# Two halves of the tokens in turn: the order of matmuls in the split products of a decoder trunk

## The chip, the cores and the metric

The kernel runs on one core of one Trainium2 chip. The metric is the device time of one execution in microseconds (us), lower is better; the median of several runs is given. The profile is one execution taken by the hardware profiler. TensorE (PE in the rows, PEld for its weight loads) multiplies, VectorE (DVE), ScalarE (ACT) and GpSimd (POOL) do the rest, SyncE (SP) issues most transfers.

## What is computed

Two residual layers over 256 tokens of 2048 features, all in float32. Cut to the parts that matter here:

```
for l in range(2):
    shift1, scale1, gate1, shift2, scale2, gate2 = split(silu(c) @ ada_w[l] + ada_b[l], 6)
    h = rms(x, norm1_g[l]) * (1 + scale1) + shift1
    mix = even_mixer(h) if l == 0 else mla_mixer(h)     # each with an input and an output projection
    x = x + gate1 * mix
    h = rms(x, norm2_g[l]) * (1 + scale2) + shift2
    x = x + gate2 * (square(relu(h @ mlp_w1[l])) @ mlp_w2[l])    # 2048 -> 8192 -> 2048
```

## The kernel before

Tokens are taken as two halves (`NH = 2`) of 128, the partitions of a PSUM tile; a product gives `[256, 512]` as two PSUM tiles of 128 x 512, one bank for each half. The features that are summed over come in blocks of 128.

**Split products.** From the even layer's output projection on, every product of activations and weights is made of three matmuls per block, half and chunk: both operands are split into a high and a low part (`split`, L93), and high x high, high x low and low x high are added in the same bank. A weight tile of four blocks x 512 columns (1 MiB) is fetched by SyncE (`wraw`, L112), copied to its high part by ScalarE (L94) and subtracted to its low part by VectorE (L95), or by GpSimd for a few tiles at the start of a stage (`self.first`). Three buffers hold high parts, two hold low parts. The even layer's input projection uses whole float32 passes instead (`gemm32`, L148).

**Order of the matmuls.** `gemm_part` (L172) takes one weight tile (or two). Its outer loop is over the halves of the tokens; inside, the four blocks, and for each block the three products at L183 (high x high), L184 (the same block of x with the low part of the weights) and L185 (low part of x, high part of the weights). So twelve matmuls add to the first half's bank and then twelve to the second's. `gemm` (L162) runs it for a whole sum. With `skew` the last two tiles go together, 24 matmuls for the first half and then 24 for the second; that is used at the last chunk of the two MLPs and of the odd layer's output projection (`at_end`, L319). With `between` (the query product, L847) other work stands between the two halves. At the start of an MLP, `gemm_quarter` (L190) and `unit_halves` (L201, products at L210 to L212) add a quarter of the features to three chunks as soon as the modulation has made that quarter; for the first quarter two chunks go together, first half first.

**Around it.** After a unit of 512 hidden channels the MLP takes relu (L452, ScalarE), a product (L454, VectorE), four transposes on TensorE (L107) and a split, for each half. After an output projection comes the residual (L411, L412), the sum of squares (L340), the norm (L345 to L354), transposes and the modulation (L380 to L383), which gives the next product's x. In the odd layer the query input's rows are squared (L656), normalized (L672) and modulated into `cT` (L678). Beside all this the conditioning is worked off step by step on VectorE (L237, L269, L297), as `side_work` (L136) doles it out per weight tile. PSUM has four banks for running sums (two units), two for transposes and two for other uses; at the start of an MLP these last two hold the third chunk.

The framework puts the instructions of each engine into a queue when the kernel is built, by the order in which they are written and by when it expects their inputs; the engine then takes its queue as it is.

Of the kernel before, what the change touches and what calls it, by code (L numbers as in the profile page):

```python
# [16 lines left out]
P = 128  # L17
# [25 lines left out]
class Trunk:  # L43
    def __init__(self, ctx, tc, t):
# [17 lines left out]
        self.first = 0  # tiles still to be split by GpSimd  # L62
# [5 lines left out]
    def rsqrt(self, out, v):  # L68
        """out = v ** -0.5 for v > 0: a first guess from the bits, a third-order step, a Newton step."""
# [14 lines left out]
        # out <- 8/3 of its third-order step, then Newton with the 8/3 taken out again  # L84
# [7 lines left out]
    def split(self, src, hi, lo, engine=None):  # L92
        """src = hi + lo, both with the 12 significant bits that one pass of the array takes."""  # L93
        self.nc.scalar.copy(hi, src)  # L94
        (engine or self.nc.vector).tensor_tensor(lo, src, hi.bitcast(F32), op=ALU.subtract)  # L95
# [6 lines left out]
    def transpose4(self, srcs):  # L102
        """Up to four [128, n] blocks -> one PSUM bank, transposed side by side."""
# [20 lines left out]
    def wtile(self, w, k0, nk, n0, nw):  # L124
# [3 lines left out]
        # VectorE is busy with the norm when a phase's first tiles come: GpSimd splits those  # L128
# [6 lines left out]
    def side_work(self, size=1.0):  # L135
        """Work that is spread beside the weight tiles: conditioning and the convolution."""  # L136
# [10 lines left out]
    def gemm32(self, ps, x, w, g, n0):  # L147
        """ps += x[:, 512 features of group g] @ w[those, n0:n0+512], whole float32 passes."""  # L148
# [12 lines left out]
    def gemm(self, x, xk0, w, k0, nkb, n0, nw, skew=False):  # L161
        """[256, nw] = x[:, K] @ w[K, n0:n0+nw], as two PSUM tiles of 128 tokens; with skew the  # L162
        first half of the tokens is complete well before the second."""
# [7 lines left out]
    def gemm_part(self, ps, x, xk0, w, k0, g, nkb, n0, nw, tiles=1, between=None):  # L171
        nc = self.nc  # L172
        xh, xl = x
        ws = [self.wtile(w, k0 + g + 4 * i, min(4, nkb - g - 4 * i), n0, nw) for i in range(tiles)]
        for h in range(NH):
            o = ps[h][:, :nw]
            for k in range(g, min(g + 4 * tiles, nkb)):
                first, last = k == 0, k == nkb - 1
                hi, lo = ws[(k - g) // 4]
                i = (k - g) % 4  # L180
                a = xh[:, xk0 + k, h * P : (h + 1) * P]
                b = xl[:, xk0 + k, h * P : (h + 1) * P]
                nc.tensor.matmul(o, a, hi[:, i, :nw], start=first, stop=False)  # L183
                nc.tensor.matmul(o, a, lo[:, i, :nw], start=False, stop=False)  # L184
                nc.tensor.matmul(o, b, hi[:, i, :nw], start=False, stop=last)  # L185
            if between and h == 0:
                between()

    def gemm_quarter(self, units, x, q, paired):
        """512 features of x into each of units = (psum, w, n0, nw); with paired, the first half of  # L190
        the tokens of two units goes before their second half."""
# [8 lines left out]
    def unit_halves(self, units, ws, x, q):  # L200
        nc = self.nc  # L201
        xh, xl = x
        for h in range(NH):
            for (ps, _, _, nw), (hi, lo) in zip(units, ws):
                o = ps[h][:, :nw]
                for i in range(4):
                    k = 4 * q + i
                    a = xh[:, k, h * P : (h + 1) * P]
                    b = xl[:, k, h * P : (h + 1) * P]
                    nc.tensor.matmul(o, a, hi[:, i, :nw], start=k == 0, stop=False)  # L210
                    nc.tensor.matmul(o, a, lo[:, i, :nw], start=False, stop=False)  # L211
                    nc.tensor.matmul(o, b, hi[:, i, :nw], start=False, stop=k == KB - 1)  # L212

# [1 line left out]
    # mod = silu(c) @ ada_w + ada_b, one 1 MiB piece of ada_w to a step  # L215
    def ada_finish_col(self, out, layer, j, q, acc):
        """Feature-major column sums of acc [128, 512], plus the bias."""
# [7 lines left out]
    def ada_col(self, layer, j):  # L225
        """self.mod[layer, j] = [128, 16], feature-major."""
# [19 lines left out]
    def ada_quarters(self, layer, j0, side=None, aided=0):  # L246
        """Columns j0 and j0 + 1 side by side, complete for 512 features after every eight steps.
        The first aided quarters go by ScalarE and GpSimd, with room for products in side."""
# [29 lines left out]
    def ada_row(self, layer, j, side=None):  # L278
        """self.mod[layer, j] = [128, 2048], the same in every partition. With side = [128, 4096],
        the products go to ScalarE and the sums to GpSimd."""  # L280
# [37 lines left out]
    def at_end(self, last):  # L318
        """Before the last product of a stage: no more work beside it."""  # L319
# [3 lines left out]
    def ada_more(self, rate, *lists):  # L323
        """Steps to be worked off beside the coming weight tiles, rate steps to a tile."""
# [26 lines left out]
    def norm_t(self, h, q, r):  # L351
        """Four blocks of (x * r).T in PSUM."""
# [4 lines left out]
    def norm_start(self, layer, which):  # L357
        """A function that gives 512 features' (shift, gain) columns: modulate(rms(x) * g) = x * rstd * gain + shift."""
# [14 lines left out]
    def norm_quarter(self, quarter, q, pair):  # L373
        """512 features of h.T, as (hi, lo)."""
# [649 lines left out]
```

## Time and profile before

| | |
|---|---|
| median of 3 runs | 2189.13 us (2187.72 to 2189.61) |
| span of the profiled execution, first to last instruction | 2185.9 us |
| what the median has beyond that span | 3.2 us |
| instructions in the span | 23655 |
| mean granted TensorE clock | 0.987 of 2.4 GHz |
| TensorE busy | 96% of the span |
| VectorE busy | 72% |
| ScalarE busy | 43% |
| read from HBM | 564.06 MB, 259 GB/s |

The profile gives the span of the profiled execution and no separate time for it, so the runs' median stands beside it. The stages in the span: conditioning and the even layer's input up to about 310 us, its output projection to 411, the first MLP to 1153, the odd layer to 1450, the second MLP to the end. TensorE's rows are matmuls with their start; they overlap, so a row's duration (0.39 us) is longer than the distance to the next start. A row of the timeline gives the start, the duration, the engine, the line, the operation and its tiles, and in brackets the idle time before it on its engine with what ended that.

### The profile page before, as it was taken

What the parts mean: (1) busy time and instruction counts of PE and PEld (TensorE: products, weight loads), DVE (VectorE), ACT (ScalarE), POOL (GpSimd) and SP (SyncE); (2) the same over time, 40 slices, a digit from 0 to 9 for tenths busy, and PEclk for the clock granted to TensorE, in tenths of its full rate; (3) what the DMA queues carried; (4) which work ended last, traced back from release to release, by engine and by line L of the source; (5) the groups of instructions that cost most, each with busy time, mean ns of one, the idle gap of its engine ahead of it and who ended that gap; (6) DMA issues with size and microseconds to landing.
All of it is one profiled execution on the core that took longest, in us unless ns stands there. A gap on an engine that the chain in (4) does not pass through costs nothing.

```text
span 2185.9 us, 23655 instructions
## 1 busy us (share of the span) xinstructions
PE 2090.9 (96%) x9138; PEld 1635.7 (75%) x9138; DVE 1564.9 (72%) x1763; ACT 932.3 (43%) x1184; POOL 146.7 (7%) x95
## 2 busy tenths in 40 slices
PE   2889999899999999999998999989999999999999
PEld 1444458678888888888888787868888888888887
DVE  6849999888777878787767878766656545554555
ACT  2135435444444334333436776444434433433432
POOL 0038710000000000000001000010000000000000
PEclk9999999899999999999999999989999999999999
DMA  9999968899898899989755646647778556556653
GB/s 350 384 346 330 332 242 295 275 317 339 315 337 315 329 326 319 339 304 334 270 174 174 211 158 214 229 154 250 256 271 264 178 192 189 189 192 192 189 191 122
DMA packets 238620, 567.70 MB, mean 260 GB/s; under 512 B 9150, under 2 KB 17784, under 8 KB 221864
## 3 DMA queue, kind: packets, MB, share of 16 engines
q1 hardware_dynamic: 236288, 562.60, 74.3%
q10 hardware_dynamic: 1564, 2.28, 0.3%
q8 instruction: 72, 1.18, 0.2%
q0 software_dynamic: 656, 1.31, 0.2%
q14 instruction: 40, 0.33, 0.0%
HBM read 564.06 MB, written 2.10 MB: 259 GB/s over the span
## 4 chain that ended last, share of the span: by engine, by line
PE 85%; DVE 9%; DMA 5%; ACT 1%; issue 1%; SPq 0%; ACTq 0%; DVEq 0%
PE mm L183 23%; PE mm L184 23%; PE mm L185 23%; PE mm L153 4%; DMA raw<-in_ada_w 4%; PE trp L107 3%; DVE accq L269 2%; DVE cvsq L542 1%; DVE wl L95 1%; PE mm L210 1%; PE mm L211 1%; PE mm L212 1%; PE sc L797 1%; PE sc L796 1%; DMA raw<-in_mlp_w 1%
## 5 line engine op out<-in xcount | busy, mean ns | idle before, releaser
L95 DVE TENSOR_TENSOR wl<-raw,wh 128x2048 fp32r<-128x2048 f32 (+2 forms) x312 | 704.7, 2259 | 424.0 <-PE mm L184 317.9
L94 ACT CAST wh<-raw 128x2048 fp32r<-128x2048 f32 (+3 forms) x316 | 596.6, 1888 | 774.1 <-PE mm L185 515.2
L183 PE MATMUL mm<-wh,f_h 128*128 128x512 f32 x1024 | 399.6, 390 | 0.0
L185 PE MATMUL mm<-wh,f_l 128*128 128x512 f32 x1024 | 399.3, 390 | 0.0
L184 PE MATMUL mm<-wl,f_h 128*128 128x512 f32 x1024 | 398.7, 389 | 0.0
L185 PE MATMUL mm<-wh,h_l 128*128 128x512 f32 (+2 forms) x928 | 358.2, 386 | 0.0
L183 PE MATMUL mm<-wh,h_h 128*128 128x512 f32 (+2 forms) x928 | 358.2, 386 | 0.0
L184 PE MATMUL mm<-wl,h_h 128*128 128x512 f32 (+2 forms) x928 | 357.0, 385 | 0.6 <-DVE wl L95 0.6
L185 PEld LDWEIGHTS mm<-wh,f_l 128*128 128x128 f32 x1024 | 192.2, 188 | 39.8
L184 PEld LDWEIGHTS mm<-wl,f_h 128*128 128x128 f32 x1024 | 192.3, 188 | 39.6
L183 PEld LDWEIGHTS mm<-wh,f_h 128*128 128x128 f32 x1024 | 192.3, 188 | 39.2
L184 PEld LDWEIGHTS mm<-wl,h_h 128*128 128x128 f32 x928 | 175.0, 189 | 34.0 <-DVE wl L95 1.1
L185 PEld LDWEIGHTS mm<-wh,h_l 128*128 128x128 f32 x928 | 174.9, 188 | 33.4
L183 PEld LDWEIGHTS mm<-wh,h_h 128*128 128x128 f32 x928 | 175.0, 189 | 32.7
L153 PE MATMUL mm<-raw,x 128*128 128x512 f32 x448 | 195.7, 596 | 1.0 <-ACT x L500 0.6
L269 DVE SCALAR_TENSOR_TENSOR accq<-raw,cT,accq 128x512 f32<-128x512 f32 x210 | 153.7, 749 | 16.6 <-DMA raw<-in_ada_w 13.3
L153 PEld LDWEIGHTS mm<-raw,x 128*128 128x128 f32 x448 | 84.6, 191 | 104.6 <-issue 98.5
L237 DVE SCALAR_TENSOR_TENSOR acc<-raw,cT,acc 128x2048 f32<-128x2048 f32 x60 | 140.8, 2346 | 9.7 <-DMA raw<-in_ada_w 9.7
L297 DVE SCALAR_TENSOR_TENSOR acc<-raw,cT,acc 128x2048 f32<-128x2048 f32 x48 | 112.7, 2347 | 4.4 <-DMA raw<-in_ada_w 4.4
L542 DVE SCALAR_TENSOR_TENSOR cvsq<-yp,convw,cvsq 128x256 f32<-128x256 f32 x240 | 96.0, 476 | 0.0
L303 POOL TENSOR_TENSOR side<-side 128x1024 f32<-128x1024 f32 x32 | 74.8, 2361 | 19.3 <-ACT side L302 19.3
L452 ACT ACTIVATE relu<-mm 128x512 f32<-128x512 f32 x60 | 35.8, 599 | 87.7 <-PE mm L185 81.5
(270 smaller groups left out, 2246.9 us busy)
## 6 DMA issues: line engine op xcount, KB each, us to landing
raw<-in_mlp_w SPq DMA_DIRECT2D x256, 1024.0 KB, 5.6
raw<-in_ada_w SPq DMA_DIRECT2D x192, 1024.0 KB, 5.4
raw<-in_ab_w_in SPq DMA_DIRECT2D x32, 1024.0 KB, 9.7
raw<-in_ab_w_out SPq DMA_DIRECT2D x16, 1024.0 KB, 8.3
raw<-in_mla_w_out SPq DMA_DIRECT2D x16, 1024.0 KB, 4.9
raw<-in_mla_w_ukv SPq DMA_DIRECT2D x8, 1024.0 KB
raw<-in_mla_w_uq SPq DMA_DIRECT2D x8, 768.0 KB, 4.8
raw<-in_mla_w_in SPq DMA_DIRECT2D x4, 1024.0 KB, 7.2
```

The costliest lines, as they stand in the source:

```text
L94: self.nc.scalar.copy(hi, src)
L95: (engine or self.nc.vector).tensor_tensor(lo, src, hi.bitcast(F32), op=ALU.subtract)
L107: self.nc.tensor.transpose(ps[:w, i * P : i * P + s.shape[0]], s, self.ident[: s.shape[0], : s.shape[0]])
L153: self.nc.tensor.matmul(ps[h], x[:, 4 * g + k, h * P : (h + 1) * P], raw[:, k, :], start=g + k == 0, stop=4 * g + k == KB - 1,)
L183: nc.tensor.matmul(o, a, hi[:, i, :nw], start=first, stop=False)
L184: nc.tensor.matmul(o, a, lo[:, i, :nw], start=False, stop=False)
L185: nc.tensor.matmul(o, b, hi[:, i, :nw], start=False, stop=last)
L237: nc.vector.scalar_tensor_tensor(acc, raw, self.cT[:, kb : kb + 1], acc, op0=ALU.mult, op1=ALU.add)
L269: self.last = nc.vector.scalar_tensor_tensor(acc, raw[:, k, :], c, acc, op0=ALU.mult, op1=ALU.add).ins
L297: nc.vector.scalar_tensor_tensor(acc, raw, c, acc, op0=ALU.mult, op1=ALU.add)
L303: nc.gpsimd.tensor_tensor(acc[:, sl], acc[:, sl], prod, op=ALU.add)
L542: nc.vector.scalar_tensor_tensor(o, y, wk, o, op0=ALU.mult, op1=ALU.add)
```

## The change

In `gemm_part` the loop over the halves moves inside the loop over blocks: for each block the three products are issued for both halves in turn. Where two tiles go together or something stands between the halves, the halves stay apart as before. `unit_halves` loops over the four blocks, then over the chunks, then over the products and halves, so the halves are in turn there too, also for the first quarter. A new function `products` holds the three products. Comments and docstrings are dropped in the changed file as well.

```diff
     def gemm_part(self, ps, x, xk0, w, k0, g, nkb, n0, nw, tiles=1, between=None):
-        nc = self.nc
-        xh, xl = x
         ws = [self.wtile(w, k0 + g + 4 * i, min(4, nkb - g - 4 * i), n0, nw) for i in range(tiles)]
-        for h in range(NH):
-            o = ps[h][:, :nw]
-            for k in range(g, min(g + 4 * tiles, nkb)):
-                first, last = k == 0, k == nkb - 1
-                hi, lo = ws[(k - g) // 4]
-                i = (k - g) % 4
-                a = xh[:, xk0 + k, h * P : (h + 1) * P]
-                b = xl[:, xk0 + k, h * P : (h + 1) * P]
-                nc.tensor.matmul(o, a, hi[:, i, :nw], start=first, stop=False)
-                nc.tensor.matmul(o, a, lo[:, i, :nw], start=False, stop=False)
-                nc.tensor.matmul(o, b, hi[:, i, :nw], start=False, stop=last)
-            if between and h == 0:
+        ks = range(g, min(g + 4 * tiles, nkb))
+        for halves in ([0], [1]) if between or tiles > 1 else ([0, 1],):
+            for k in ks:
+                hi, lo = (w[:, (k - g) % 4, :nw] for w in ws[(k - g) // 4])
+                self.products([ps[h][:, :nw] for h in halves], x, xk0 + k, hi, lo, halves, k == 0, k == nkb - 1)
+            if between and halves == [0]:
                 between()
 
+    def products(self, outs, x, k, hi, lo, halves, first, last):
+        for i, (a, w) in enumerate(((0, hi), (0, lo), (1, hi))):
+            for o, h in zip(outs, halves):
+                self.nc.tensor.matmul(
+                    o, x[a][:, k, h * P : (h + 1) * P], w, start=first and i == 0, stop=last and i == 2
+                )
+
...
     def unit_halves(self, units, ws, x, q):
-        nc = self.nc
-        xh, xl = x
-        for h in range(NH):
+        for i in range(4):
             for (ps, _, _, nw), (hi, lo) in zip(units, ws):
-                o = ps[h][:, :nw]
-                for i in range(4):
-                    k = 4 * q + i
-                    a = xh[:, k, h * P : (h + 1) * P]
-                    b = xl[:, k, h * P : (h + 1) * P]
-                    nc.tensor.matmul(o, a, hi[:, i, :nw], start=k == 0, stop=False)
-                    nc.tensor.matmul(o, a, lo[:, i, :nw], start=False, stop=False)
-                    nc.tensor.matmul(o, b, hi[:, i, :nw], start=False, stop=k == KB - 1)
+                k = 4 * q + i
+                outs = [ps[h][:, :nw] for h in range(NH)]
+                self.products(outs, x, k, hi[:, i, :nw], lo[:, i, :nw], range(NH), k == 0, k == KB - 1)
```

## Rows read from the trace of the kernel before

**Rows 1.** The page, part 1: busy us, share of the span and instructions of each engine

```profile
PE 2090.9 (96%) x9138; PEld 1635.7 (75%) x9138; DVE 1564.9 (72%) x1763; ACT 932.3 (43%) x1184; POOL 146.7 (7%) x95
```

**Rows 2.** Windows: stretch, its us, busy PE PEld DVE ACT POOL, clock, DMA, GB/s

```profile
411.00:422.50 11.50, 1.29 (x6) 0.74 (x5) 11.00 (x32) 5.11 (x10) 0.00 (x0) 0.67 0.97 330
414.95:428.60 13.65, 7.21 (x22) 5.68 (x23) 11.23 (x35) 7.04 (x15) 0.00 (x0) 0.50 0.78 247
508.00:1153.00 645.00, 645.00 (x2917) 533.10 (x2916) 499.46 (x326) 259.79 (x198) 6.96 (x7) 1.00 0.86 306
1532.00:2181.00 649.00, 649.00 (x2924) 536.24 (x2922) 355.87 (x231) 258.98 (x189) 0.00 (x0) 1.00 0.62 204
```

**Rows 3.** Groups of instructions: count, busy us, mean ns, idle before; two weight loads of the MLPs

```profile
L183 PEld LDWEIGHTS mm<-wh,f_h 128*128 128x128 f32 x1024 | 192.3, 188 | 39.2
L184 PEld LDWEIGHTS mm<-wl,f_h 128*128 128x128 f32 x1024 | 192.3, 188 | 39.6
```

**Rows 4.** Timeline of TensorE in the first MLP (start us, us, engine, line, operation)

```profile
797.64 0.39 PE L184 MATMUL mm<-wl,h_h 128*128 128x512 f32 x1
...
812.15 0.39 PE L185 MATMUL mm<-wh,h_l 128*128 128x512 f32 x1
812.37 0.39 PE L183 MATMUL mm<-wh,h_h 128*128 128x512 f32 x1
...
813.96 0.39 PE L184 MATMUL mm<-wl,h_h 128*128 128x512 f32 x1
```

**Rows 5.** Timeline of all engines there: relu of the first half, transposes of both

```profile
812.57 0.60 ACT L452 ACTIVATE relu<-mm 128x512 f32<-128x512 f32 x1 [4.61 <-PE mm L185]
...
815.33 0.60 PE L107 MATMUL trp<-ident,sq 128*128 128x128 f32 x4
...
820.12 0.60 PE L107 MATMUL trp<-ident,sq 128*128 128x128 f32 x4
```

**Rows 6.** Timeline, end of the even output projection and start of the first MLP

```profile
408.77 0.68 DVE L411 TENSOR_TENSOR rt<-mm,gate 128x512 f32<-128x512 f32 x1
...
410.79 0.39 PE L185 MATMUL mm<-wh,cat_l 128*128 128x512 f32 x1
...
419.13 1.08 PE L107 MATMUL trp<-ident,xn 128*128 128x128 f32 x4 [7.95 <-DVE nr L87]
...
422.48 0.80 PE L210 MATMUL mm<-wh,h_h 128*128 128x512 f32 x1 [2.26 <-DVE h_h L382]
...
426.19 0.43 DVE L382 CAST h_h<-full 128x512 fp32r<-128x512 f32 x1 [1.71 <-ACT full L380]
```

**Rows 7.** Groups of instructions on VectorE from 411 to 422.5 us

```profile
L269 DVE SCALAR_TENSOR_TENSOR accq<-raw,cT,accq 128x512 f32<-128x512 f32 x7 | 5.2, 747 | 0.0
```

**Rows 8.** Timeline, odd layer: square of the query input's first half, first query product

```profile
1215.60 0.60 ACT L656 ACTIVATE rj<-mm 128x512 f32<-128x512 f32 x1 [1.23 <-PE mm L185]
...
1228.19 0.44 PE L183 MATMUL mm<-wh,cT 128*128 128x384 f32 x1 [0.69 <-DVE cT L678]
```

**Rows 9.** Timeline, first MLP: the two waits for the low part of the weights

```profile
481.88 0.51 PE L211 MATMUL mm<-wl,h_h 128*128 128x512 f32 x1 [1.59 <-DVE wl L95]
...
507.35 0.50 PE L184 MATMUL mm<-wl,h_h 128*128 128x512 f32 x1 [0.64 <-DVE wl L95]
```

**Rows 10.** Timeline, start of the second MLP: first matmuls, cast of the second half

```profile
1462.59 0.78 PE L210 MATMUL mm<-wh,h_h 128*128 128x512 f32 x1
1463.16 0.63 PE L211 MATMUL mm<-wl,h_h 128*128 128x512 f32 x1
1463.59 0.63 PE L210 MATMUL mm<-wh,h_h 128*128 128x512 f32 x1
...
1464.58 0.43 DVE L382 CAST h_h<-full 128x512 fp32r<-128x512 f32 x1 [1.05 <-ACT full L380]
```

**Rows 11.** Timeline, start of the odd layer's input product, cast of the second half

```profile
1162.00 0.61 PE L183 MATMUL mm<-wh,h_h 128*128 128x320 f32 x1
...
1164.27 0.43 DVE L382 CAST h_h<-full 128x512 fp32r<-128x512 f32 x1 [1.33 <-ACT full L380]
```

## The prediction

> **What bounds the kernel now.** I read the busy times first: TensorE is busy for 96% of the span, and it loads weights exactly as often as it multiplies, 9138 times [rows 1]. Then the stretches: in the two channel MLPs, from 508 to 1153 and from 1532 to 2181 us, TensorE is busy for 645.00 of 645.00 and 649.00 of 649.00 us at full clock, while VectorE has 77% and 55% and the DMA engines 86% and 62% [rows 2]. Nothing there makes TensorE wait, so in these 1294 us (59% of the span) only its own rate counts. It stands idle at the seams between stages. Between 411 and 422.5 us it works for 1.29 us while VectorE is busy for 11.00 of 11.50, and the clock is at its lower level, 0.50 of 2.4 GHz, from 414.95 to 428.60 [rows 2]. So there are two questions: does the new order change the time of one matmul, and does it make a seam longer or shorter?
>
> The page's span is 2185.9 us, against a median of 2189.13: 3.2 us lie before the first and after the last instruction. I make the sum on the span and add these 3.2 again. A measurement of this kernel can tell some 0.2%, 4.4 us, from no change.
>
> **Part 1, the rate of matmuls.** By the loops 7584 matmuls have three products (two MLPs 6144, the two output projections 768, the latent attention's input 288 and its two low-rank products 384). 336 of these keep their order, because the three stage ends and the query product still take the halves apart, so the change touches 7248. It neither adds nor removes one; each has its own weight load before and after. Two loads in a row that bring the same block of x (L183 and L184) take 188 ns each [rows 3], so nothing was saved by having them next to each other, and nothing is lost when they are parted: 0 us.
>
> The price of staying in one bank can be read in the kernel before, which changes bank after every twelfth matmul. From 797.64 to 813.96 us there are 72 intervals, 16.32 us, 226.7 ns each, and six of them go from one half's bank to the other's [rows 4]. One such change can be placed: ScalarE starts the relu of the first half at 812.57 us, as soon as that half's last matmul (812.15) is done [rows 5]; the next one, at 812.37, is thus the first of the second half's last twelve. It starts 0.22 us after its neighbour, like the others within the rounding (0.23) [rows 4]. At 2.4 GHz 512 columns are 213.3 ns, so each interval has 13.3 ns more than the columns alone. If same-bank additions made this, the interval at the change would be 0.21. A gain or loss per bank change lies between 0 and the rounding of these starts, 0.01 us either way; I take 0, because the six intervals with a change leave the mean of the 72 at that of their neighbours. Part 1: 0 us.
>
> **Part 2, results come later.** The first half's sum was complete 12 matmuls, 12 x 0.2267 = 2.7 us, before the second's; now both end together, when the second did. In the MLPs this hides: the transposes that follow the relu run at 815.33 and 820.12 us [rows 5], in the midst of the next unit's 96 matmuls (21.8 us), and a later pair only moves within them. Each pair of banks is free again long before the unit after next needs it. If that cover were gone, each of the 32 units would pay up to 2.7 us, 87 us in all; I cost it at 0.
>
> Two places have less cover. (a) At the end of the even layer's output projection, whose last chunk has no special order of halves, the residual of the first half starts at 408.77 us, while TensorE goes on to 410.79 [rows 6]. It will start after 411.18, 2.4 us later, and it heads the chain residual, sum of squares, norm, transposes, that TensorE waits for until 419.13 (7.95 us) and again until 422.48 [rows 6]. VectorE is full in that stretch [rows 2], and 5.2 us of it are seven partial sums of the conditioning [rows 7], which can go first instead. So between 0 and +2.4 us; I take the middle, +1.2. (b) After the query input of the odd layer, the first half's square (0.60 us on ScalarE) ran at 1215.60 beside the second half's matmuls [rows 8]; now it is in line ahead of the second's, and the reciprocal root needs both. TensorE already waits there (0.69 us at 1228.19 [rows 8]): 0 to +0.8, with its read of the sum, and I take +0.8, as this wait has no cover.
>
> **Part 3, the low part of the weights is needed later.** Of each block the order was hi, lo, hi; now it is hi, hi, lo, lo, hi, hi. The first use of lo is the third matmul of a tile, not the second, and its last use the 22nd of 24, not the 23rd. Where TensorE waited for lo, 1.59 us at 481.88 and 0.64 us at 507.35 [rows 9], it does one more matmul first: 2 x -0.23 = -0.5 us. VectorE gets the lo buffer 0.23 us earlier for its next subtraction, and nothing else is queued behind a new wait there: 0.
>
> The transfers themselves stay as they are: the weight tiles are asked for in the same order and count, and a raw buffer is released by the split, not by a matmul. SP's and GpSimd's queues are passed by nothing. What moves is only which product of a tile comes first.
>
> **Part 4, the starts of stages.** Where a stage starts, the second half of the features is not ready when the first is. By the new loops the second matmul already needs it. The gap from the first matmul to the end of the second half's cast (row plus its duration) is 422.48 to 426.62 in the first MLP [rows 6], 1462.59 to 1465.01 in the second [rows 10], and 1162.00 to 1164.70 at the odd layer's input [rows 11]: 4.1 + 2.4 + 2.7 = 9.2 us. But the order on the engine is not that of the program's lines. In the second MLP the program issues L210, L211, L212 and repeats; TensorE runs L210, L211, L210 [rows 10]. The framework that orders the queue takes what it expects to be ready, over several banks. Then it can still run the first half's products while the second half is late. I take 0, with 0 to +9.2 as ends and the longer time at half clock below.
>
> Sum: 0 + 1.2 + 0.8 - 0.5 + 0 = +1.5 us on 2185.9, with the 3.2 us around it 2190.6 us.
>
> **The rivals.** *The second matmul of a stage waits (slower).* Place: the three starts of part 4. Price: up to 9.2 us of waiting, and if the clock's return to 2.4 GHz, which in the first MLP came 6.1 us after its first matmul (422.48 to 428.60) [rows 2, 6], is put off as long, 9.2 us more run at half rate and lose up to 4.6 us. With (a) at its full 2.4 and (b) at 0.8, 2189.1 + 3.2 + 9.2 + 4.6 = 2206 at most, 2199 for half of the waits. It decides from the point where a second-half matmul stands in TensorE's queue ahead of ready ones. Against it speaks the mixed order [rows 10]; for it, that this order is fixed beforehand by expected times, and TensorE can't pass a waiting matmul: at 481.88 it stands 1.59 us at an lo product [rows 9], though the next one needs only hi, which was there from the matmul before. The Trainium skill (PSUM — Partial Sum Buffer, Engine vs sequencer instructions) says the same: matmuls start and complete in program order. By that rule every misplaced second-half product costs its whole wait, and the trace agrees, with the 1.59 us. 0.25.
>
> *The bank does matter (faster).* If the 13.3 ns over the bare columns went away, 7248 x 13.3 ns = 96 us at most (some products have fewer columns), 2093 us. The bank changes speak against it [rows 4]. The Trainium skill (TensorE: Matmul & The Clock Gate, Back-to-back issue gap) gives N/2.4 + 2.5 ns for a single matmul's gap, 215.8 ns for 512 columns; by an estimate from it the 7248 would take 79 us less. The trace disagrees: 226.7 ns. 0.02.
>
> *A luckier order of the queues (faster).* The seam from 411 to 422.5 us holds 10.2 us without TensorE work [rows 2], and every instruction beside the changed products is ordered anew. That seam cut by half gives -5 us, 2184. Nothing in the rows points to it beyond the VectorE work that can move ahead in (a). 0.11.
>
> *No change that can be told* is the forecast, 0.62.
>
> **How the numbers follow.** The forecast's own range is 2188 to 2193: 2189.1 - 0.5 with (a) and (b) at 0, and 2192.3 with both at their upper ends and a little of the starts. The slower case reaches from 2194 to 2206; half of its 0.25 lies above 2199. The faster cases, 0.13, lie mostly just under 2185, with about 0.07 below 2184. From 2184 to 2199 us thus leaves out 0.07 + 0.125, under 2 in 10. Faster by over 0.2%: 0.13; within: 0.62; slower: 0.25.
>
> **What would show it.** Right: matmuls of 512 columns still start 226.7 ns apart in a dense stretch, both relus of a unit follow each other, and both MLP stretches stay full. Part 2: the first residual at the end of the output projection starts after the last matmul there. Part 3: two hi products ahead of each wait for lo. Part 4: in the three starts TensorE runs several products of one half before the other's cast ends; if instead it waits after the first one, the slower rival holds. An interval under 220 ns in the dense stretches would make the whole prediction wrong.

## The result and the profile after

The changed kernel takes 2196.31 us (median of 6 runs, 2194.59 to 2199.38); the kernel before took 2188.53 beside it (6 runs). The ratio is 1.0034 with a 95% interval from 1.0022 to 1.0045: slower by 0.34%, 7.8 us. The forecast was 2190.6 us with 2184 to 2199 as its range. The range holds the time, but "no change that can be told" was taken as likeliest, and the change can be told. The profiled execution took 2196.58 us with a span of 2194.8, so 1.8 us lie around a span. The 3.2 us that the prediction added to a span held another 1.4 us, by which that profiled execution was shorter than the median.

The page, part 1, of the changed kernel: busy us, share of the span, instructions.

```profile
PE 2095.8 (95%) x9138; PEld 1636.0 (75%) x9138; DVE 1561.9 (71%) x1763; ACT 930.6 (42%) x1184; POOL 147.1 (7%) x95
```

The counts are those of [rows 1]; nothing was added. TensorE's busy time grew by 4.9 us, the span by 8.9, so some 4 us are standing still and the rest is in matmuls that took longer. The stretches (columns as in [rows 2], with one added) say where:

```profile
411.00:422.50 11.50, 0.61 (x4) 0.22 (x3) 11.15 (x32) 3.55 (x6) 0.00 (x0) 0.70 0.97 343
422.50:508.00 85.50, 79.29 (x345) 64.04 (x345) 68.33 (x73) 35.30 (x50) 1.80 (x1) 0.92 0.79 273
508.00:1153.00 645.00, 645.00 (x2921) 532.04 (x2921) 498.83 (x325) 263.34 (x202) 4.36 (x6) 1.00 0.87 306
1532.00:2181.00 649.00, 649.00 (x2918) 533.87 (x2917) 358.88 (x233) 261.51 (x194) 0.00 (x0) 1.00 0.62 205
```

The dense stretches are as full as they were. In the 85.5 us between them and the even layer TensorE is busy for 79.29 us at a mean clock of 0.92; in the kernel before it was 82.94 us at 0.96. In the dense part the rate is unchanged, two rows of TensorE's timeline (x2: a pair that goes to the two halves' banks):

```profile
797.25 0.62 PE L186 MATMUL mm<-wh,f_h 128*128 128x512 f32 x2
...
805.41 0.62 PE L186 MATMUL mm<-wh,h_h 128*128 128x512 f32 x2
```

There are 36 matmuls in these 8.16 us: 226.7 ns each, to the digit what [rows 4] gave, although now every one adds to another bank than the one before it.

To find the places I lined up the two traces at the same matmul, counting those that write a tile named mm. The offset of the changed kernel is +0.05 us at the 672nd (395 us, in the even output projection), +1.69 at the 768th (434 us, just into the first MLP), +6.18 at the 1056th (532 us, its start is over), +7.01 at the 3648th (1139 us), +7.32 at the 4992nd (1543 us, dense part of the second MLP) and +8.88 at the end. So there are three places: the **seam** after the even layer (+1.64), the **first MLP's start** (+4.49), and a **slow drift** in the dense parts (+0.83 and +1.55); 0.31 us lie between.

The seam, timelines of VectorE and TensorE:

```profile
407.65 2.29 DVE L95 TENSOR_TENSOR wl<-raw,wh 128x2048 fp32r<-128x2048 f32 x1 [0.33 <-ACT wh L94]
411.35 2.29 DVE L95 TENSOR_TENSOR wl<-raw,wh 128x2048 fp32r<-128x2048 f32 x1 [1.41 <-ACT wh L94]
413.56 0.68 DVE L405 TENSOR_TENSOR rt<-mm,gate 128x512 f32<-128x512 f32 x1
...
410.85 0.61 PE L186 MATMUL mm<-wh,cat_l 128*128 128x512 f32 x2
422.35 2.22 PE L107 MATMUL trp<-ident,xn 128*128 128x128 f32 x8 [10.88 <-DVE r L90]
425.49 0.79 PE L186 MATMUL mm<-wh,h_h 128*128 128x512 f32 x1 [0.92 <-DVE h_h L376]
```

The first residual comes not 2.4 but 4.8 us later than in [rows 6] (413.56 against 408.77): a weight tile's subtraction, 2.29 us, slipped ahead of it in VectorE's queue. TensorE waits 10.88 us for the transposes instead of 7.95, and the first MLP begins 3.0 us later. At 434 us only 1.64 us of that are left. Both kernels begin this MLP at half clock, and it comes back at nearly the same time in both (428.6 and 429.3 us), so starting 3.0 us earlier was worth about half of that.

The first MLP's start, where the third quarter of features meets its second tile: VectorE, ScalarE, TensorE in the changed kernel.

```profile
468.20 0.43 DVE L376 CAST h_h<-full 128x512 fp32r<-128x512 f32 x1 [1.24 <-ACT full L374]
468.60 2.35 DVE L291 SCALAR_TENSOR_TENSOR acc<-raw,cT,acc 128x2048 f32<-128x2048 f32 x1
472.64 0.43 DVE L376 CAST h_h<-full 128x512 fp32r<-128x512 f32 x1 [1.09 <-ACT full L374]
474.43 2.29 DVE L95 TENSOR_TENSOR wl<-raw,wh 128x2048 fp32r<-128x2048 f32 x1 [1.36 <-ACT wh L94]
...
471.11 1.50 ACT L374 ACTIVATE full<-trp,mod,A 128x128 f32<-128x128 f32 x4 [2.94 <-PE trp L107]
472.49 3.70 ACT L94 CAST wh<-raw 128x2048 fp32r<-128x2048 f32 x2
...
470.41 0.60 PE L107 MATMUL trp<-ident,xn 128*128 128x128 f32 x4
474.45 1.22 PE L186 MATMUL mm<-wh,h_h 128*128 128x512 f32 x2 [3.20 <-ACT wh L94]
476.25 1.22 PE L186 MATMUL ms<-wh,h_h 128*128 128x512 f32 x2 [0.57 <-ACT wh L94]
477.27 1.05 PE L186 MATMUL mm<-wl,h_h 128*128 128x512 f32 x2
```

And the same tile in the kernel before:

```profile
463.32 1.92 ACT L94 CAST wh<-raw 128x2048 fp32r<-128x2048 f32 x1 [5.88 <-DMA raw<-in_mlp_w]
465.14 0.45 ACT L380 ACTIVATE full<-trp,mod,A 128x128 f32<-128x128 f32 x1
...
465.27 2.29 DVE L95 TENSOR_TENSOR wl<-raw,wh 128x2048 fp32r<-128x2048 f32 x1 [1.57 <-ACT wh L94]
467.48 0.42 DVE L382 CAST h_h<-full 128x512 fp32r<-128x512 f32 x1
```

Read the order, not the durations. Before, the tile's rounding (wh) stood ahead of the last quarter's scale-and-shift (full) on ScalarE, and its subtraction (wl) ahead of that quarter's casts (h_h) on VectorE. Now both stand behind. ScalarE waits 2.94 us at a full for transposes that TensorE has behind its matmuls at 470.41, while the tile, asked for at 459.89 us, waits (its landing isn't in the trace; the kernel before asked for this tile at 457.40 us and rounded it 5.9 us later); the subtraction comes at 474.43, not 465.27; TensorE stands 3.20 and 0.57 us, and after that a pair takes 0.85 us (477.27 to 478.12 and on), not 0.45: the lower clock. The same 6.83 us in the changed kernel and then in the kernel before (columns as in the windows above):

```profile
473.68:480.51 6.83, 5.48 (x12) 3.90 (x13) 6.08 (x4) 2.52 (x2) 0.00 (x0) 0.50 0.60 197
473.68:480.51 6.83, 6.28 (x26) 4.35 (x24) 6.08 (x4) 1.91 (x1) 0.00 (x0) 1.00 1.00 326
```

So the +4.49 us have two parts. TensorE's waits of over 0.1 us between the 768th and the 1056th matmul add up to 5.24 us, against 2.53 in the kernel before: +2.7. The other 1.8 us go with the granted clock, 0.50 in this stretch where the kernel before had 1.00: 12 matmuls against 26.

The drift, one unit of the second MLP (VectorE, then TensorE):

```profile
1674.41 2.29 DVE L95 TENSOR_TENSOR wl<-raw,wh 128x2048 fp32r<-128x2048 f32 x1 [3.15 <-PE mm L186]
1676.62 0.68 DVE L448 TENSOR_TENSOR sq<-mm,relu 128x512 f32<-128x512 f32 x1
...
1677.45 0.63 PE L107 MATMUL trp<-ident,sq 128*128 128x128 f32 x4
```

The first half's relu now comes when the next tile's subtraction has already started, its square sq waits behind that, and the transposes find it not ready: the interval before them is 0.35 us, not 0.23. Of the intervals ahead of such transposes after 532 us, 21 are over 0.30 us in the changed kernel and 1 in the kernel before; some 0.12 us each, 2.4 us together.

### The profile page after: what moved, and what is told of

It is laid out like the page before. It is cut to its first block, busy times and chain, and to the rows that moved or that the text cites. A ratio compares the mean times of both kernels' runs of the same rounds, so it can differ in the third digit from the quotient of the medians.

```text
span 2194.8 us, 23657 instructions
## 1 busy us (share of the span) xinstructions
PE 2095.8 (95%) x9138; PEld 1636.0 (75%) x9138; DVE 1561.9 (71%) x1763; ACT 930.6 (42%) x1184; POOL 147.1 (7%) x95
## 5 line engine op out<-in xcount | busy, mean ns | idle before, releaser
L186 PE MATMUL mm<-wh,h_h 128*128 128x512 f32 (+2 forms) x1056 | 327.5, 390 | 4.1 <-ACT wh L94 3.2
L186 PE MATMUL mm<-wl,h_h 128*128 128x512 f32 (+2 forms) x1056 | 326.5, 388 | 1.5 <-DVE wl L95 1.5
L186 PE MATMUL mm<-wh,h_l 128*128 128x512 f32 (+2 forms) x1056 | 324.9, 386 | 0.0
L186 PE MATMUL mm<-wl,f_h 128*128 128x512 f32 x1024 | 319.8, 390 | 0.0
L186 PE MATMUL mm<-wh,f_h 128*128 128x512 f32 x1024 | 319.0, 390 | 0.0
L186 PE MATMUL mm<-wh,f_l 128*128 128x512 f32 x1024 | 318.5, 389 | 0.0
L186 PEld LDWEIGHTS mm<-wh,h_h 128*128 128x128 f32 x1056 | 196.9, 190 | 41.8 <-ACT wh L94 3.5
L186 PEld LDWEIGHTS mm<-wh,h_l 128*128 128x128 f32 x1056 | 198.1, 189 | 39.1
L186 PEld LDWEIGHTS mm<-wl,h_h 128*128 128x128 f32 x1056 | 197.2, 190 | 39.5 <-DVE wl L95 1.9
L186 PE MATMUL mm<-wh,cT 128*128 128x512 f32 (+1 forms) x256 | 74.0, 375 | 0.7 <-DVE cT L672 0.7
```

The lines of the kernel that those rows point to most:

```text
L186: self.nc.tensor.matmul(o, x[a][:, k, h * P : (h + 1) * P], w, start=first and i == 0, stop=last and i == 2)
```

## The experiments

The theory at the start: seam 3.2 us, first MLP's start 3.0 us because both first tiles are held to the end of 48 matmuls, relus 2.2 us, second start 0.5 us. The table gives each run's steps in us between the five matmuls named above, each against the kernel before, and the ratio of the times.

| kernel | seam | start | dense 1 | odd layer | dense 2 | ratio [95%] |
|---|---|---|---|---|---|---|
| changed | +1.64 | +4.49 | +0.83 | +0.31 | +1.55 | 1.0034 [1.0022, 1.0045] |
| e1 | +0.66 | +0.74 | +0.68 | +0.33 | +1.47 | 1.0032 [1.0020, 1.0043] |
| e12 (e1 again) | +2.59 | +1.85 | +0.80 | +0.11 | +1.47 | 1.0017 [1.0008, 1.0026] |
| e2 | +0.64 | +3.91 | +0.08 | -1.41 | -0.03 | 1.0013 [1.0004, 1.0022] |
| e3 | -0.40 | +4.77 | +0.89 | +0.49 | +1.61 | 1.0032 [1.0021, 1.0043] |
| e4 | +1.24 | +4.37 | +4.53 | -0.22 | +1.49 | 1.0042 [1.0029, 1.0056] |
| e5 | -0.32 | +4.89 | -0.03 | +0.96 | -0.02 | 1.0023 [1.0013, 1.0033] |
| e6 | -2.05 | +0.31 | +0.92 | +0.47 | +0.01 | 1.0005 [0.9996, 1.0014] |
| e7 | -0.75 | +2.35 | -0.05 | -0.97 | +0.05 | 1.0016 [1.0007, 1.0025] |
| e8 | +1.47 | +2.69 | +0.76 | -0.51 | +1.51 | 1.0038 [1.0025, 1.0051] |
| e9 | -0.46 | +4.64 | +0.96 | -0.06 | +0.05 | 1.0014 [1.0005, 1.0023] |
| e11 | +0.42 | +5.35 | +0.16 | +0.18 | +0.08 | 1.0018 [1.0008, 1.0028] |
| e15 | -0.83 | -2.89 | +0.27 | -0.01 | 0.00 | 0.9990 [0.9981, 0.9999] |

A step is from one execution, and executions of one kernel differ by a few us; a column tells most where all kernels of a kind agree. e1 and e12 are one kernel, and their seams differ by 1.9 us, their starts by 1.1. The column of the odd layer, which holds the second MLP's start too, goes from -1.41 to +0.96 without a pattern. The kernel before took 2186.57 us beside e1 to e4, 2187.52 beside e5 to e8, 2188.40 beside e9 to e12 and 2188.47 beside e15, so times of different groups are compared by the ratio.

**e1: the old order in `unit_halves`, in turn elsewhere.**

```diff
     def unit_halves(self, units, ws, x, q):
-        for i in range(4):
+        for h in range(NH):
             for (ps, _, _, nw), (hi, lo) in zip(units, ws):
-                k = 4 * q + i
...
+                for i in range(4):
```

> The changed kernel with the old order in unit_halves alone (the first half's products of both units, then the second half's); every other sum still goes by halves in turn. My theory: the changed kernel lost its time at four places, read by aligning the two traces at the same matmul: 3.2 us at the end of the even output projection, 3.0 us at the first MLP's start (both first tiles are held to the end of 48 matmuls), 0.1 us for each unit whose transposes follow a relu (about 2.2 us over both MLPs), 0.5 us at the second MLP's start. Then this kernel keeps the first and the third and loses the second and fourth: offset against the kernel before +3.2 at the first MLP's first matmul, still about +3.2 (not +6.2) at its 1056th matmul, and a time 3.5 us under the changed kernel's, about 2193. Rival: the 3.0 us at the first MLP's start follow from its late start alone (other due times, other order of VectorE's queue); then the offset there is +6 as in the changed kernel and the time 2196.

Measured: 2193.86 us. The ratio, 1.0032, can't be told from the changed kernel's 1.0034, where the theory wanted 3.5 us less. In the profiled execution the start's step is +0.74, which points to `unit_halves`; but that execution (2190.95) was the fastest of its six, and its seam cost only 0.66. Whether that was chance is e12's question.

**e2: the new order in `unit_halves` alone**, put into the kernel before (the diff's last hunk and `products`).

> The kernel before with the new order in unit_halves alone; all other sums as before. My theory: the end of the even projection and the units' relus are as before (offset 0 at the first MLP's first matmul, no slope along the dense stretches), and the first MLP's start loses 3.0 us by itself, the second's 0.5: 2188.5 + 3.5 = 2192. Rival (the loss there follows from the late start): offset 0 at the end too, 2188.5.

Measured: 2189.89 us, start +3.91, dense parts +0.08 and -0.03. The loss at the start is there without any late start, and the time is 3.3 us over that of the kernel before beside it, as the theory had it; in the profiled execution 1.41 us come back in the odd layer.

**e3: halves apart in the last tile of the even projection's last chunk.**

```diff
-        for halves in ([0], [1]) if between or tiles > 1 else ([0, 1],):
+        for halves in ([0], [1]) if between or tiles > 1 or (self.apart and g + 4 == nkb) else ([0, 1],):
```

(`self.apart` is set around that chunk alone.)

> The changed kernel with the halves apart again in the last tile of four blocks of the even output projection's last chunk alone. My theory: the first residual starts at 408 to 409 us again, before the last matmul there, TensorE's wait for the transposes is 7.9 us again, not 10.9, and the first MLP's first matmul comes at 422.5, not 425.5; the rest stays, so about 3.0 us under the changed kernel, 2193. Rival (this lateness is absorbed later, since VectorE and the transfers bound the first MLP's start): the first matmul comes earlier, but the offset after its 1056th matmul is +6 as in the changed kernel, 2196.

Measured: 2194.69 us. The first residual starts at 410.07 us, before the last matmul there, TensorE's wait is 8.08 us, and the seam goes from +1.64 to -0.40: 2.0 us, not 3.0, because of the clock as above. The start's step stays at +4.77; it is not lateness carried on. So in this execution the theory's 3.0 us are 2.0, and the rival's "absorbed" isn't borne out; the ratios, 1.0032 and 1.0034, don't show the gain.

**e4: one unit after the other, halves in turn.**

```diff
-        for i in range(4):
-            for (ps, _, _, nw), (hi, lo) in zip(units, ws):
+        for (ps, _, _, nw), (hi, lo) in zip(units, ws):
+            for i in range(4):
```

> The changed kernel with another order in unit_halves: all 24 matmuls of the first unit, halves in turn, then the 24 of the second, so that the first unit's two tiles come free after 24 of 48 matmuls instead of after 42 (36 in the kernel before). Theory (it is the tiles held to the end, and VectorE's subtractions queued for them, that cost the 3.0 us at the first MLP's start): at least 3 us less than the changed kernel, 2193 or under. Rival (the order of halves at the start costs it, a second-half product ahead of ready ones): this order needs both halves just as early, so 2196 or more.

Measured: 2198.57 us, start +4.37. The theory of the held tiles falls: the first tiles came free early (the subtraction that waits for them runs at 432.74 us, not at 437.80 as in the changed kernel) and the step is the same. The time is as the rival had it; e9 takes that rival up. In this execution, one of three near 2198.6 us (the other two took 2193.4 and 2194.5), the first dense part lost 4.53 us, most of it at three intervals of 1.3 to 1.5 us before transposes of sq between 647 and 697 us. e6 has one such interval (1.13 us, at 635.6) and e9 two shorter ones (0.74 and 0.42 us, at 638.4 and 661.3), though their sums end with the halves apart; these make up nearly all of their first dense steps of +0.92 and +0.96. What brings these on stays open.

**e5: halves apart in the last tile of every sum. e6: the same, with the old `unit_halves`.**

```diff
-        for halves in ([0], [1]) if between or tiles > 1 else ([0, 1],):
+        for halves in ([0], [1]) if between or g + 4 * tiles >= nkb else ([0, 1],):
```

> The changed kernel with the halves apart again in the last tile (four blocks) of every sum, in turn everywhere else, the new order in unit_halves kept. Theory (what is lost along the two MLPs, 2.3 us in the changed kernel between its 1056th matmul and its end outside the seams, comes from the transposes behind a relu, of which the first half's is no longer 12 matmuls ahead): the offset against the kernel before stays flat along both dense stretches, as it did where only unit_halves was new, and the step at the first MLP's start stays, +4 to +6; time 2 to 3 us under the changed kernel's. Rival (the in-turn order itself is slower in dense work, by some 0.3 ns a matmul): the offset grows by 2 us as before.

> As the run above, and the old order in unit_halves: in turn in all tiles of all sums but the last, and not at the MLPs' starts. Theory: nothing of the loss is left: offset under 0.7 us at the end, time within 1.5 us of the kernel before. Rival (in-turn products cost by themselves): some 2 us slower.

Measured: e5 2191.12, e6 2188.46 us. In e5 the drift is gone (-0.03 and -0.02). Here is the unit of the last fence again, in e5 (ScalarE, VectorE, TensorE):

```profile
1669.73 0.60 ACT L446 ACTIVATE relu<-mm 128x512 f32<-128x512 f32 x1 [0.80 <-PE mm L186]
...
1670.36 0.69 DVE L448 TENSOR_TENSOR sq<-mm,relu 128x512 f32<-128x512 f32 x1 [1.46 <-ACT relu L446]
1672.23 2.29 DVE L95 TENSOR_TENSOR wl<-raw,wh 128x2048 fp32r<-128x2048 f32 x1 [1.17 <-PE mm L186]
...
1672.26 0.60 PE L107 MATMUL trp<-ident,sq 128*128 128x128 f32 x4
```

The square is done before the subtraction starts, and the transposes run without a wait. Of all intervals before such transposes 2 are over 0.30 us. e6 keeps most products in turn, and its interval holds no change (its upper end is 1.0014, 3 us): alternating banks by itself shows no cost. Its offset at the end, +0.94 us against the under 0.7 that was expected, is that one interval at 635.6 us. Between e5 and e6 only `unit_halves` differs: its new order costs 2.66 us in the medians, ratio 1.0023 against 1.0005.

**e7 and e8: order edges.** In e2's kernel (e7) and the changed kernel (e8) the last quarter's full, h_h and the acc traced beside it were queued behind the third quarter's second tile, as before.

```diff
+                if layer == 0 and q == 3:
+                    for a in self.late:
+                        for b in (self.casts[1], self.subs[1]):
+                            if a.ins.engine == b.ins.engine:
+                                self.tc.add_manual_dep(a.ins, b.ins.name, ...)
```

> The kernel before with the new order in unit_halves alone (the second run's kernel, offset +4.1 us after the 1056th matmul), and order edges at one place: the scale-and-shift and the casts of the last quarter of features, and the partial sums traced beside it, are queued behind the rounding and the subtraction of the third quarter's second tile, as they stood in the kernel before. No matmul moves by that. Theory: the step at the first MLP's start is not the matmuls' order itself but that ScalarE's and VectorE's queues were ordered anew by it, so that this tile's lo part came at 471.3, not 465.3 us, TensorE ran dry at 469 us and its clock fell: here TensorE doesn't stand over 1.5 us at 469 to 472 us, its clock stays at full there, and the offset after the 1056th matmul is +1 us or less; time about 2188. Rival (second-half products that stand ahead of ready ones cost it): still +3.5 us or more, 2190.

> The changed kernel with the same order edges. Theory: its step at the first MLP's start, +6.2 us after the 1056th matmul, falls to +2 us or less; what it loses behind the relus stays, so about +4.5 us at the end, time about 2191 to 2192. Rival (late start and products out of turn cost it): still +5 us or more there, time 2195.

Measured: 2189.82 and 2195.11 us. The standstill near 470 us goes in both, but the start's step falls only from 3.91 to 2.35 and from 4.49 to 2.69. The offsets at the 1056th matmul are +2.13 in e7, between theory and rival, and +5.74 in e8, which is the rival's side; both times are the rivals', and the ratios (1.0016 against e2's 1.0013, 1.0038 against 1.0034) show no gain from the edges. In e8 the clock stays at 1.00 from 431 to 532 us, but the waits there still add up to 4.76 us. In e7 the wait moved to the next tile, TensorE:

```profile
473.51 0.61 PE L205 MATMUL ms<-wh,h_h 128*128 128x512 f32 x2
476.42 0.73 PE L205 MATMUL ms<-wl,h_h 128*128 128x512 f32 x2 [2.29 <-DVE wl L96]
```

There TensorE's own queue had the transposes later (468.03 us, 464.47 in the kernel before), so full and the casts came late, and the third tile's subtraction behind them at 474.08. Two queues put back is not three.

**e9: one unit after the other, halves apart**, in the kernel before; no products in turn anywhere.

```diff
-        for h in range(NH):
-            for (ps, _, _, nw), (hi, lo) in zip(units, ws):
+        for (ps, _, _, nw), (hi, lo) in zip(units, ws):
+            for h in range(NH):
```

> The kernel before with one edit in unit_halves: the loop over units outside the loop over halves. No products are in turn anywhere; the halves stay apart, and the first unit's tiles come free after 24 matmuls instead of 36. In the order of the queues the subtraction of the third quarter's second tile then stands behind the casts of the last quarter of features and a partial sum, as in the changed kernel, not ahead of them as in the kernel before. Theory (the step at the first MLP's start is that order of ScalarE's and VectorE's queues, whatever brings it about): TensorE stands 2.5 us or more near 470 us and the offset after the 1056th matmul is +3 us or more, time 2190 to 2192, though no half waits for the other. Rival (products in turn, second half's among the first's, make the step): offset 0 or less there, time 2187.

Measured: 2191.46 us, start +4.64. VectorE and TensorE in e9:

```profile
465.32 2.35 DVE L297 SCALAR_TENSOR_TENSOR acc<-raw,cT,acc 128x2048 f32<-128x2048 f32 x1 [0.81 <-DMA acc<-in_ada_b]
468.51 0.43 DVE L382 CAST h_h<-full 128x512 fp32r<-128x512 f32 x1 [0.24 <-ACT full L380]
470.30 2.29 DVE L95 TENSOR_TENSOR wl<-raw,wh 128x2048 fp32r<-128x2048 f32 x1 [1.36 <-ACT wh L94]
...
466.28 0.60 PE L107 MATMUL trp<-ident,xn 128*128 128x128 f32 x4
470.32 1.22 PE L210 MATMUL mm<-wh,h_h 128*128 128x512 f32 x2 [3.21 <-ACT wh L94]
```

The same picture as in the changed kernel, with the same 3.2 us. So such a step needs no halves in turn: another order of the units is enough to plan the queues like this. That it is the order of ScalarE's and VectorE's queues, rather than TensorE's own, is argued from these rows; e7 and e8 didn't show it.

**e11: e9 with the order edges of e7.**

> As the run above, with the order edges (the last quarter's scale-and-shift, casts and partial sums behind the third quarter's second tile). Theory: the standstill near 470 us goes and most of the step with it, offset after the 1056th matmul +1.5 us or less; if the earlier release of the first tiles is worth something, it is under 0 and this kernel is the fastest, 2186. Rival: as the run above.

Measured: 2192.77 us, start +5.35: a miss. In place of the 3.2 us there are four waits of 0.58 to 1.16 us between 463 and 479 us, and the clock fell at 487 us besides. Edges at one place don't mend this; edges that put all three queues back were not tried.

**e12: e1's kernel again.**

> The kernel of the first run once more (products in turn in all sums, old order in unit_halves), for a second profiled execution: the first was the fastest of its six, 2190.95 against a median of 2193.86, and its offset of +3.25 us at the end explains no more than that. Theory (the late end of the even projection, +2.1 us at its transposes there, is absorbed at the first MLP's start in some executions only): in an execution near the median the offset after the 1056th matmul is +3 us or more, with a long wait or half clock between 425 and 531 us. Rival (it is lost elsewhere): the offset there is under 1.5 us again and the rest shows at another place.

Measured: 2193.70 us; the offset at the 1056th matmul is +3.98, with seam +2.59 and start +1.85, as the theory had it. The instructions of TensorE, VectorE and ScalarE are in the same order as in e1; the clock differs. Windows of e1 (busy PE, PEld, DVE, ACT, POOL, clock, DMA, GB/s):

```profile
425.00:428.00 3.00, 3.00 (x12) 2.44 (x11) 2.31 (x5) 1.70 (x5) 0.00 (x0) 0.59 0.51 187
428.00:431.00 3.00, 3.00 (x17) 2.48 (x16) 2.47 (x6) 1.55 (x5) 0.00 (x0) 1.00 0.00 0
485.00:489.00 4.00, 4.00 (x19) 3.32 (x18) 4.00 (x4) 2.61 (x3) 0.00 (x0) 1.00 1.03 381
```

and of e12:

```profile
425.00:428.00 3.00, 2.35 (x8) 1.96 (x9) 2.84 (x7) 1.71 (x6) 0.00 (x0) 0.50 0.89 304
428.00:431.00 3.00, 3.00 (x12) 2.31 (x11) 2.22 (x5) 1.32 (x4) 0.00 (x0) 0.58 0.04 12
485.00:489.00 4.00, 4.00 (x12) 3.14 (x11) 3.00 (x2) 1.17 (x2) 0.00 (x0) 0.57 1.05 415
```

Full clock came back before 428 us in e1 and near 431 in e12, and after the same interval of 1.99 us without a matmul, from 480.4 and 482.4 us, the clock stayed full in e1 and fell in e12 (19 matmuls against 12 in four us). Whether a late seam is absorbed differs from execution to execution.

**e15: e5 with competing work moved away.** The conditioning's second list, the acc products, is traced after the first MLP's start.

```diff
-        self.ada_more(R2, self.ada_row(0, 5), *(self.ada_col(1, j) for j in (0, 1, 3)), gate[:16])
+        self.later = (R2, self.ada_row(0, 5), *(self.ada_col(1, j) for j in (0, 1, 3)), gate[:16])
...
+        if layer == 0:
+            self.ada_more(*self.later)
```

> The fifth run's kernel (products in turn but in the last tile of every sum, new order in unit_halves; step of +4.6 us between the even layer's output projection and the 1056th matmul, flat after it), with the conditioning's second list (the partial sums named acc: a 1 MiB transfer and a 2.35 us product on VectorE each) traced after the first MLP's start, not beside its tiles; the same work follows later in that MLP. Theory (at the start TensorE waits for the lo parts of its tiles, and the new order loses there because VectorE's queue and the transfers have the sums and the features' casts ahead of them): the sixth subtraction comes 4 us earlier or more than in that run, the step falls to +1.5 us or less, and, if the later sums find room in the dense stretch (VectorE has 77% there, the transfers 86%), the time is that of the kernel before or up to 2 us under it, 2186 to 2188; if they don't, TensorE shows new waits for lo between 550 and 1153 us. Rival (the products in turn make the step themselves): step +4 us or more, time 2191 or more.

Measured: 2186.04 us against 2188.47, ratio 0.9990 [0.9981, 0.9999]: a tenth of a per cent faster than the kernel before, with the interval's end just short of 1, and 0.3% under e5's ratio. The start's step is -2.89, not +4.89. ScalarE and VectorE in e15:

```profile
459.99 1.91 ACT L94 CAST wh<-raw 128x2048 fp32r<-128x2048 f32 x1 [0.78 <-DMA raw<-in_mlp_w]
465.37 1.51 ACT L374 ACTIVATE full<-trp,mod,A 128x128 f32<-128x128 f32 x4 [3.47 <-DVE A L361]
...
462.72 2.29 DVE L95 TENSOR_TENSOR wl<-raw,wh 128x2048 fp32r<-128x2048 f32 x1
466.91 0.43 DVE L376 CAST h_h<-full 128x512 fp32r<-128x512 f32 x1 [1.24 <-ACT full L374]
```

The second tile's rounding and subtraction are ahead of full and h_h again, at 459.99 and 462.72 us, and TensorE shows no interval over 0.34 us from 462 to 500 us. The dense part took the later sums at +0.27 us. This run changes two things at once: less work in the stretch, and with it another planned order. It shows that with the new order in `unit_halves` the start need lose nothing once tiles and subtractions come in time; how much of that is load and how much order it doesn't separate, and the same move in the kernel before was not run, so what the new order would cost there is open.

## Why the prediction was right or wrong

- **Part 1, rate: right.** 226.7 ns per matmul with a change of bank every time; e6 shows no cost of it. The rival "the bank does matter" is dead. The 215.8 ns that the prediction took from the Trainium skill (TensorE: Matmul & The Clock Gate, Back-to-back issue gap) is that section's gap of an isolated matmul; in this stream of weight loads and matmuls the rows show 226.7.
- **Part 2 (a), the seam: right in kind, a little short.** It took +1.2 out of 0 to 2.4, from a residual 2.4 us later. Over the executions, those with the last tile in turn (changed, e1, e12, e4, e8) have a mean seam of +1.5 and those with it apart (e2, e3, e5, e6, e7, e9, e11, e15) of -0.5: about 2 us. The "which can go first instead" of the conditioning's seven partial sums failed: seven still run between 414 and 422.5 us, after the first residual, and a weight tile's subtraction went first. The residual was 4.8 us late, TensorE's first matmul 3.0, and the half clock took the edge off.
- **Part 2, the MLP units: the step that failed second.** "A later pair only moves within them", costed at 0, looked at the transposes' place and not at what the square would meet on VectorE. It meets the next tile's 2.29 us subtraction: 0.12 us at 21 places, 2.4 us measured, 0 when the last tile is apart (e5). The second dense part bears this out in every run (+1.5 to +1.6 with the last tile in turn, at most 0.08 with it apart), the first in all but e6 and e9, with their few longer intervals, and e4.
- **Part 2 (b): wrong, harmlessly.** TensorE's wait at the query product is 0.70 us, at 1235.17 us, against 0.69 in [rows 8]; the +0.8 didn't come.
- **Part 3: wrong, by half a microsecond.** It took the order of the program's lines for TensorE's. In the kernel before two hi products stood ahead of both waits already, ahead of the 0.64 us at 507.35 [rows 9] as ahead of the 1.59:

```profile
479.56 0.73 PE L210 MATMUL mm<-wh,h_h 128*128 128x512 f32 x2
...
506.01 0.71 PE L183 MATMUL mm<-wh,h_h 128*128 128x512 f32 x2
```

  So there was nothing to gain: in e1, with that sum in turn, the second wait is 0.62 us. Its "the weight tiles are asked for in the same order" held (the 543 transfers that SyncE issues come in the same order); "nothing else is queued behind a new wait there" was false of ScalarE's and VectorE's queues.
- **Part 4, the starts: the step that failed first.** It looked at the first matmuls of each start and took 0. That was right there: TensorE starts at least three first-half products in each of the three stages before the second half's cast is done, as "what would show it" had it. The cost came 45 us later, at the third quarter's second tile: 3.9 to 4.9 us in the four kernels with that loop order (changed, e2, e3, e5), 4.4 and 4.6 in the two with other new ones (e4, e9), against 0.3 to 1.9 with the old one (e1, e6, e12). The rival "the second matmul of a stage waits" had the right stage, a price of up to 9.2 us and the wrong mechanism: not a half that waits for the other, but tiles that come late out of queues planned anew, and the half clock behind that wait; e9 has both with no halves in turn. Which of the queues would have to go back stays open (e7, e8, e11). It drew on the order of TensorE's queue alone; the section of the Trainium skill that it names (PSUM — Partial Sum Buffer, Engine vs sequencer instructions) says that ScalarE's and VectorE's queues are strictly first in, first out, and the trace agrees: the rounding at 472.49 us stands behind a full that waited 2.94 us. By that rule "every instruction beside the changed products is ordered anew" should have stood under the slower cases with a price, not under "a luckier order" alone.
- **The sum.** +1.5 forecast; measured 1.64 + 4.49 + 0.83 + 0.31 + 1.55, with 0.05 before them 8.9 us in the profiled executions, 7.8 in the medians. With the last tiles apart and the old starts (e6) 0.94 us of both are left. The base, 2189.1, is the median of three runs; over six it is 2188.53. That the range holds 2196.31 us is luck: its upper part came from half of the waits of the slower rival, and those didn't come.

## What to carry to other kernels

A loop order on one engine is also an order for the queues of the engines that feed it: before costing an edit at nothing, name for each engine what the moved instruction will meet in line, as here the square behind a 2.29 us subtraction. In this kernel taking the halves in turn is free inside a sum and costs at its end, because the earlier half is what the next step's work hides behind; so keep the halves apart in the last tile. Where a stretch lives on tiles arriving just in time, moving work that can wait out of it was worth more (2.9 us gained where 4.9 were lost, in one execution each; 1.0023 to 0.9990 in the ratios) than ordering edges at one place, which gained nothing that the times show.

## What was unexpected

The same instructions in the same order give spans some us apart, by the clock: in e1 and e12 (2189.2 and 2192.3 us) TensorE had the same interval of 1.99 us near 481 us, and the granted clock in the four us after 485 was 1.00 in one and 0.57 in the other. A start 3.0 us earlier was worth 1.6 us, as full clock came back at nearly the same time in both kernels.
